# A two-block transformer layer on one core: the second block in three groups of tiles instead of two, its weights read three times

## The chip, the cores and the metric

The kernel runs on one core of a Trainium2 chip. The metric is the device time of one execution in microseconds; the median of three runs before the change is 2220.45 us. Five engines work side by side: TensorE (PE, matrix products; its weight loads are listed as PEld), VectorE (DVE), ScalarE (ACT), GpSimd (POOL, which here issues the gathers) and SyncE (SP, which issues the other transfers).

## The reference, cut to what matters

The input is 512 tokens of width 1024, float32. The first block ends in a layer that looks up experts; the second block is a projection, two mixers and an output product:

```python
# first block, last layer: for each token 8 heads x 16 experts = 128 rows of u and of v
uc = u[ic]
act = jnp.einsum("cd,ced->ce", xc, uc)
hid = gelu(act) * gc
return jnp.einsum("ce,ced->cd", hid, v[ic])
...
# second block
proj = rmsnorm_2(x, norm_pre) @ w_in                      # 1024 x 6416
xbc, dt_raw, z_ssd, sc_h, sc_b, sc_c, z_sc = split(proj)
xbc = silu(causal_dwconv(xbc, ssd_conv_w, ssd_conv_b))    # 4 taps along the tokens
y_ssd = rmsnorm_2(ssd_chunked(xbc, softplus(dt_raw + dt_bias), ...) * silu(z_ssd), ssd_norm)
y_sc = sc_b * causal_dwconv(sc_c * sc_h, sc_conv_w) * silu(z_sc)
x = x + rmsnorm_2(concatenate([y_ssd, y_sc]) @ w_out, norm_post)
return x + sigmoid(x @ w_ple_gate) * (p_i @ w_ple_proj)
```

The scan `ssd_chunked` runs over chunks of 128 tokens and carries a state from one chunk to the next, and both convolutions carry a few last columns, so the second block takes the token tiles in order.

## The kernel before, in words

The 512 tokens are four tiles of 128. Attention and the first block's products come first; the second block's own begin at 1185.6 us, when the gathers of tiles 0 and 1 are through. The expert rows are fetched by 512 gathers (line 269), one per tile and expert slot: each brings 128 rows of 2048 numbers, 1.049 MB, into one of six buffers `g`. VectorE multiplies the u half with the tokens and sums (line 271), ScalarE takes the gelu (276), VectorE builds two small diagonals `dg` (280), and TensorE adds the v half into `acc` (285). When a tile's 128 gathers are through, `folded` adds the sums to `xres` and sets `pre[t]`, which the second block needs to begin that tile.

The gathers are a generator, `peers`. The class `Paced` counts the columns that the other products stream, and each time `every` columns have been emitted it steps the generator once, which emits two gathers with their work; `steps_now` steps it without other work, and `drain` runs it out. Every engine works in the order of the program that a scheduler made of this, so the place of a gather's products among TensorE's other products is fixed.

The second block is `block_c(tiles)`, called for tiles 0 and 1 and, after the drain, for tiles 2 and 3. Its parts, by the names that the profile shows: `xbc` (10 blocks of 128 columns of the projection, each followed by a convolution on VectorE), `z` (8 blocks), the scan (`dt`, `acs`, `xsT`, `bm`, `cb`, `al`, `ys`, `st`, `sn`), `sc` (32 blocks in fours), `mix` (the output product, 16 blocks) and `pg` with `pp` (8 and 2 blocks). A block of weights is 512 KB, loaded by `wtile` (line 206) into one of four buffers. Except in `mix` of tiles 0 and 1 and in `pp`, `halves` splits it into two parts of a shorter format, the high part by a cast on ScalarE (353) and the low part by a subtraction on VectorE (354), and each product is three products of parts. `rows` keeps 128 x 128 of the weights stationary and streams the tokens of the group; `cols` keeps 128 tokens stationary and streams 512 columns of weights. In the second call a pool `px` adds a third buffer for the split weights and a split copy `yc` of the mixers' output.

```python
NG = 256
PACE_B, PACE_Q, PACE_C = 13600, 10500, 4600
...
block_c([0, 1])
T.drain()
gathering.close()
with pool("px") as px:
    block_c([2, 3], px)
```

Of the kernel before, what the change touches and what calls it, by code (L numbers as in the profile page):

```python
# [8 lines left out]
F32 = mybir.dt.float32  # L9
# [4 lines left out]
AF = mybir.ActivationFunctionType  # L14
# [3 lines left out]
P = 128  # L18
# [9 lines left out]
def _blocks(w, nb):  # L28
    return np.ascontiguousarray(w.reshape(8, P, nb, P).transpose(2, 1, 0, 3))


def _moving(w, n):
    k, c = w.shape
    kk = 1024 // n
    w = w.reshape(k // (kk * P), kk, P, c // n, n).transpose(3, 0, 2, 1, 4)
    return np.ascontiguousarray(w)
# [47 lines left out]
def layout(inp):  # L84
    f = {k: np.asarray(v) for k, v in inp.items()}
    g = lambda n: f[n][0]
    x = f["x"][0]
    w = g("w_in")
    w2 = g("w_in_2")
    a = {}  # L90
    a["x"] = np.ascontiguousarray(x)
    a["xT"] = np.ascontiguousarray(x.T.reshape(8, P, S).transpose(1, 0, 2))
    a["wqa"] = _blocks(w[:, 0:512], 4)
    a["wka"] = _blocks(w[:, 512:1024], 4)
    a["wva"] = _moving(w[:, 1024:1536], 512)
    a["wqb"] = _blocks(w[:, 1536:2048], 4)
    kb = w[:, 2048:2176].reshape(1024, 2, 1, 64)
    a["wkb"] = _blocks(np.broadcast_to(kb, (1024, 2, 2, 64)).reshape(1024, 256), 2)
    a["wvb"] = _blocks(w[:, 2176:2304], 1)
    a["wga"] = _blocks(w[:, 2304:3328], 8)  # L100
    a["wgb"] = _blocks(w[:, 3328:4352], 8)
    pj = np.stack([g("w_proj_a"), g("w_proj_b")])
    a["wgm"] = np.stack([_moving(w[:, 2304 + 1024 * i:3328 + 1024 * i], 512) for i in range(2)])
    a["wpm"] = np.stack([_moving(m, 512) for m in pj])
    a["wproj"] = np.ascontiguousarray(pj.reshape(2, 4, P, 8, P).transpose(3, 2, 0, 1, 4).reshape(8, P, 8, P))
    a["wout"] = _moving(g("w_out"), 512)
    a["wq"] = _blocks(g("peer_w_q"), 16)
    a["subk"] = np.ascontiguousarray(g("peer_sub_keys").reshape(16, P, P).transpose(2, 0, 1))
    a["uv"] = np.ascontiguousarray(np.concatenate([g("peer_u"), g("peer_v")], 1))
    a["nab"] = _na_bias(g("na_rpb"))  # L110
    sw = _swap()
    gq, gk = g("gqa_q_norm_g"), g("gqa_k_norm_g")
    a["gqk"] = np.ascontiguousarray(np.tile(np.stack([gq, gq[sw], gk, gk[sw]], 1), (2, 1)))
    a["n1"] = _col(g("norm1_g"))
    a["rows"] = np.ascontiguousarray(np.stack([g("norm2_g"), f["norm_f_g"], g("norm_pre_2"), g("norm_post_2")]))
    a["w2"] = _blocks(np.concatenate([w2[:, 0:1280], w2[:, 1296:]], 1), 50)
    a["wdt"] = np.ascontiguousarray(w2[:, 1280:1296].reshape(8, P, 16).transpose(1, 0, 2))
    a["cw"] = np.ascontiguousarray(g("ssd_conv_w_2").reshape(4, 10, P).transpose(2, 1, 0))
    a["cb"] = _col(g("ssd_conv_b_2"))
    a["scw"] = np.ascontiguousarray(g("sc_conv_w_2").reshape(3, 8, P).transpose(2, 1, 0))  # L120
    a["heads"] = np.ascontiguousarray(np.stack([g("dt_bias_2"), g("a_log_2")]))
    a["dsk"] = _col(np.repeat(g("d_skip_2"), 64))
    a["ssn"] = _col(g("ssd_norm_2"))
    a["wo2"] = _moving(g("w_out_2"), 512)
    a["wpg"] = _moving(g("w_ple_gate_2"), 512)
    a["wpp"] = _moving(g("w_ple_proj_2"), 512)
    p = g("p_2")[0]
    a["pT"] = np.ascontiguousarray(p.T.reshape(2, P, S).transpose(1, 0, 2))
    a.update(_tables())
    return a  # L130
# [43 lines left out]
def program(tc, a, out):  # L174
# [1 line left out]
    V, A, G, SP = nc.vector, nc.scalar, nc.gpsimd, nc.sync  # L176
    T = Paced(nc.tensor)
    first, rest = [0], [1, 2, 3]
    NG = 256
    PACE_B, PACE_Q, PACE_C = 13600, 10500, 4600  # L180

    with ExitStack() as ctx:
        cst = ctx.enter_context(tc.tile_pool(name="cst", bufs=1))
# [14 lines left out]
        def bank(name, tag="mm"):  # L198
            if tag in turns:
                turn[tag] = turn.get(tag, -1) + 1  # L200
                tag = turns[tag][turn[tag] % len(turns[tag])]
            return ps.tile([P, 512], F32, tag=tag, name=name, bufs=2 if tag in ("mm", "sb") else 1)
# [34 lines left out]
        def transpose4(dst, src):  # L237
            b = bank("tr")
            for i in range(4):
                T.transpose(b[:, i * P:(i + 1) * P], src[:, i * P:(i + 1) * P], idn)  # L240
            A.copy(dst, b.rearrange("p (a t) -> p a t", a=4))
# [606 lines left out]
        with tc.tile_pool(name="pc", bufs=1) as pc, tc.tile_pool(name="pd", bufs=2) as pd:  # L848
# [34 lines left out]
                    V.tensor_tensor(lo, b3, hi, op=OP.subtract)  # L883

            def block_c(tiles, px=None):
                n = len(tiles) * P
                last = tiles[-1] == NT - 1
                tags = ["p1", "a0", "a1"] if last else ["sb", "p1"]
                turns["mm"] = ["mm", "mm", "p0"]
# [46 lines left out]
                bT, cT = xsT[:, 8, :], xsT[:, 9, :]  # L936
                ycat = pc.tile([P, 16, NG], F32, tag="ycat", name="ycat")

                for c in range(8):
                    b = bank("z")  # L940
                    rows(a["w2"][10 + c], hT2, b, n, wws)
                    A.activation(ycat[:, c, :n], b[:, :n], AF.Tanh, scale=0.5)
                    V.scalar_tensor_tensor(ycat[:, c, :n], ycat[:, c, :n], 1.0, b[:, :n], op0=OP.add, op1=OP.mult)
# [118 lines left out]
                        A.copy(yc[:, 0, 0:8, tk], ycat[:, 0:8, tk])  # L1062
                        V.tensor_tensor(yc[:, 1, 0:8, tk], ycat[:, 0:8, tk], yc[:, 0, 0:8, tk], op=OP.subtract)

                for c in range(8):
                    bb = {}
                    for j in (0, 2, 3, 1):
                        bb[j] = bank("sc4", "mm" if j in (0, 3) else "sb")
                        rows(a["w2"][18 + 8 * j + c], hT2, bb[j], n, wws)
                    bh, bbm, bcm, bz = (bb[j] for j in range(4))  # L1070
                    hs = pd.tile([P, NG], F32, tag="hs", name="hs")
                    A.copy(hs[:, :n], bh[:, :n])
                    v = pd.tile([P, 2 + NG], F32, tag="raw", name="v")
                    V.tensor_copy(v[:, 0:2], halo2[:, c, :])
                    V.tensor_tensor(v[:, 2:2 + n], hs[:, :n], bcm[:, :n], op=OP.mult)
                    V.tensor_copy(halo2[:, c, :], v[:, n:n + 2])
                    o = ycat[:, 8 + c, :n]
                    V.tensor_scalar(o, v[:, 0:n], scw[:, c, 0:1], None, op0=OP.mult)
                    for j in range(1, 3):
                        V.scalar_tensor_tensor(o, v[:, j:j + n], scw[:, c, j:j + 1], o, op0=OP.mult, op1=OP.add)  # L1080
                    A.activation(hs[:, :n], bz[:, :n], AF.Tanh, scale=0.5)
                    V.tensor_tensor(o, o, bbm[:, :n], op=OP.mult)
                    V.scalar_tensor_tensor(hs[:, :n], hs[:, :n], 1.0, bz[:, :n], op0=OP.add, op1=OP.mult)
                    V.scalar_tensor_tensor(o, o, 0.5, hs[:, :n], op0=OP.mult, op1=OP.mult)
                    if px:
                        A.copy(yc[:, 0, 8 + c, :n], o)
                        V.tensor_tensor(yc[:, 1, 8 + c, :n], o, yc[:, 0, 8 + c, :n], op=OP.subtract)
# [31 lines left out]
                        SP.dma_start(out[t * P:(t + 1) * P, hsl], gt)  # L1119

            block_c([0, 1])
            T.drain()
            gathering.close()
            with pool("px") as px:
                block_c([2, 3], px)

# [15 lines left out]
```

## Time and profile before

| | |
|---|---|
| median of 3 runs | 2220.45 us (2219.86 to 2221.79) |
| profiled execution | 2217.67 us, of which the span is 2215.8 us |
| busy in the span | PE 1851.5 us (84%), DVE 1628.1 (73%), ACT 735.1 (33%), POOL 598.8 (27%) |
| transfers | 711.71 MB, mean 321 GB/s; the gathers' queue 536.90 MB |
| chain that ended last | PE 36%, DMA 25%, DVE 24%; largest line: the gathers' landing, 23% |

A busy share is an average over stages that have different limits, so the table does not say what a change in one stage is worth. For that the span is cut at the places where TensorE goes from one part of the second block to the next, and each stretch is read by itself: which engine or whether the transfers are full there.

### The profile page before, as it was taken

The numbers are of one execution on the slowest core, as the hardware profiler recorded it, in microseconds if no ns is written. First come the engines' busy times: TensorE is split into PE (matmuls) and PEld (weight loads), VectorE is DVE, ScalarE is ACT, GpSimd is POOL, SyncE is SP. The second block draws the span as 40 slices with busy tenths as digits, with TensorE's granted clock in tenths as the row PEclk, the third lists the DMA queues.
The fourth block names the chain that finished last, engine by engine and source line by source line (L and its number), as shares of the span: only waits on it lengthen the run. The fifth ranks groups of instructions, "written<-read, shape, count | busy, mean of one in ns | idle before, by whom it ended". The sixth has DMA issues, their size and how long they took to land.

```text
span 2215.8 us, 29509 instructions
## 1 busy us (share of the span) xinstructions
PE 1851.5 (84%) x10292; PEld 1032.5 (47%) x10292; DVE 1628.1 (73%) x4007; ACT 735.1 (33%) x1471; POOL 598.8 (27%) x520
## 2 busy tenths in 40 slices
PE   7998699899999898656648886896899866799998
PEld 5767445444444654001104552462453421298896
DVE  5376986788885966888868887886775766687865
ACT  4374265566501421111123342321220310154443
POOL 0000223333331233444433334433423333200000
PEclk9999789999999998656758997998999976699999
DMA  5366979889997899999989989899999999653363
GB/s 211 127 228 216 363 288 344 335 325 350 346 381 273 316 378 394 380 380 397 362 306 346 418 365 396 335 418 420 406 415 416 402 416 421 276 170 97 119 189 121
DMA packets 127316, 711.71 MB, mean 321 GB/s; under 512 B 15168, under 2 KB 18752, under 8 KB 61248
## 3 DMA queue, kind: packets, MB, share of 16 engines
q0 software_dynamic: 73728, 536.90, 60.6%
q1 hardware_dynamic: 53440, 172.92, 22.1%
q8 instruction: 83, 1.36, 0.2%
q14 instruction: 65, 0.53, 0.1%
HBM read 707.67 MB, written 2.10 MB: 320 GB/s over the span
## 4 chain that ended last, share of the span: by engine, by line
PE 36%; DMA 25%; DVE 24%; issue 7%; ACT 6%; POOL 1%; another core or an unknown queue 0%; DVEq 0%; POOLq 0%; ACTq 0%; SPq 0%
DMA g<-in_uv,idx 23%; DVE g L271 9%; PE sc L168 5%; PE acc L285 4%; PE mix L168 3%; PE pq L168 2%; PE ga L168 2%; PE z L168 2%; DVE dg L280 2%; PE pg L168 2%; PE ys L168 2%; DVE ww L354 2%; POOL g L269 1%; DVE own L295 1%; PE xbc L168 1%
## 5 line engine op out<-in xcount | busy, mean ns | idle before, releaser
L269 POOL DMA_INDIRECT g<-in_uv,idx x512 | 595.0, 1162 | 1297.7 <-PE acc L285 610.2
L285 PE MATMUL acc<-g,dg 64*64 64x512 f32 x3584 | 626.5, 755 | 249.9 <-DVE dg L280 229.8
L271 DVE SCALAR_TENSOR_TENSOR g<-g,xnp 128x1024 f32<-128x1024 f32 x512 | 624.7, 1221 | 188.2 <-DMA g<-in_uv,idx 181.9
L285 PEld LDWEIGHTS acc<-g,dg 64*64 64x64 f32 x3584 | 122.9, 154 | 621.0 <-DVE dg L280 492.8
L276 ACT ACTIVATE act<-act 128x1 f32<-128x1 f32 (+1 forms) x448 | 90.8, 203 | 945.7 <-DVE g L271 912.2
L354 DVE TENSOR_TENSOR ww<-w,ww 128x1024 fp32r<-128x1024 f32 x175 | 213.4, 1222 | 76.4 <-ACT ww L353 74.5
L280 DVE TENSOR_SCALAR dg<-two,act,gate 128x64 f32<-128x64 f32 x512 | 172.1, 351 | 132.6 <-ACT act L276 129.9
L353 ACT CAST ww<-w 128x1024 fp32r<-128x1024 f32 x175 | 182.2, 1044 | 172.8 <-PE sc L168 63.6
L168 PEld LDWEIGHTS sc<-hT,ww 128*128 128x128 f32 x1536 | 190.0, 193 | 54.0 <-issue 44.5
L168 PE MATMUL sc<-hT,ww 128*128 128x256 f32 x1536 | 206.1, 289 | 6.0 <-ACT fold L333 3.2
L168 PE MATMUL pq<-xT,w 128*128 128x128 f32 (+1 forms) x768 | 127.8, 323 | 0.6 <-DMA w<-in_wq 0.6
L168 PEld LDWEIGHTS pq<-xT,w 128*128 128x128 f32 x768 | 112.0, 200 | 19.8 <-issue 12.2
L295 DVE SCALAR_TENSOR_TENSOR own<-g,hid,own 128x512 f32<-128x512 f32 x127 | 95.1, 749 | 2.3
L168 PE MATMUL ga<-h,w 128*128 128x384 f32 x256 | 93.1, 513 | 2.8 <-DVE rot L411 2.8
L276 ACT ACT_TABLE_LOAD x61 | 78.3, 1283 | 18.1 <-DVE g L271 16.3
L168 PE MATMUL xbc<-hT,ww 128*128 128x256 f32 x480 | 64.2, 290 | 6.2 <-DVE ww L354 3.3
L168 PEld LDWEIGHTS xbc<-hT,ww 128*128 128x128 f32 x480 | 59.3, 192 | 20.4 <-issue 9.5
L168 PEld LDWEIGHTS ga<-h,w 128*128 128x128 f32 x256 | 48.7, 198 | 37.6 <-issue 8.3
L168 PE MATMUL q<-h,w 128*128 128x128 f32 (+1 forms) x256 | 61.1, 394 | 3.4 <-ACT rsq L407 3.4
L168 PE MATMUL mix<-w,ycat 128*128 128x512 f32 x128 | 61.5, 612 | 0.0
L168 PEld LDWEIGHTS z<-hT,ww 128*128 128x128 f32 x384 | 46.9, 190 | 12.3 <-issue 10.5
L168 PE MATMUL z<-hT,ww 128*128 128x256 f32 x384 | 50.5, 287 | 1.5 <-ACT raw L928 1.3
(338 smaller groups left out, 2269.8 us busy)
## 6 DMA issues: line engine op xcount, KB each, us to landing
w<-in_w SPq DMA_DIRECT2D x100, 512.0 KB
w<-in_wq SPq DMA_DIRECT2D x48, 512.0 KB
w<-in_wo SPq DMA_DIRECT2D x32, 512.0 KB
w<-in_wgm SPq DMA_DIRECT2D x16, 512.0 KB
w<-in_wout SPq DMA_DIRECT2D x16, 512.0 KB
g<-in_uv,idx POOLq DMA_INDIRECT x512
w<-in_wpg SPq DMA_DIRECT2D x16, 512.0 KB
w<-in_wqa SPq DMA_DIRECT2D x8, 512.0 KB
```

The source lines that it names most:

```text
L168: return self.count(max(n, 128) * (4 if rhs.dtype == F32 else 1), self.tensor.matmul(out, lhsT, rhs, **kw))
L269: G.indirect_dma_start(out=g.rearrange("p a d -> p (a d)"), out_offset=None, in_=a["uv"], in_offset=bass.IndirectOffsetOnAxis(ap=hk_idx[t] ...
L271: V.scalar_tensor_tensor(g[:, 0, :], g[:, 0, :], 1.0, xnp, op0=OP.mult, op1=OP.mult, accum_out=act[:, j % grp:j % grp + 1])
L276: A.activation(act[:, :grp], act[:, :grp], AF.Gelu)
L280: V.tensor_scalar(dg[:, m, :], two[:, 1, :], act[:, m:m + 1], gate[:, m:m + 1], op0=OP.mult, op1=OP.mult)
L285: T.tensor.matmul(acc[i][o, :], w, v, start=(e0 + j + 1 == grp), stop=(e0 + j + grp >= P), tile_position=(64 * i, 64 * m), skip_group_chec ...
L295: V.scalar_tensor_tensor(own, g[:, 1, HALVES[1]], hid[:, j:j + 1], own, op0=OP.mult, op1=OP.add)
L353: A.copy(ww[:, 0], w)
L354: V.tensor_tensor(ww[:, 1], w, ww[:, 0], op=OP.subtract)
```

## The change

`block_c` is called three times: for tiles 0 and 1, for tile 2, and for tile 3. The gathers of tile 2 are stepped at one step per 7960 columns (before: 4600) beside tiles 0 and 1 and then run until tile 2 is ready; the gathers of tile 3 are stepped at 5800 beside tile 2; what is left is drained, and tile 3 runs last, with `px`. Each call reads all of the block's weights (50 + 16 + 8 + 2 blocks of 512 KB).

In a call with one tile, `z` and `sc` go through `cols`, from a second layout of the same weights, `w2m`: 128 tokens are stationary and 512 columns of weights move. The results then have tokens on the partitions and are turned by TensorE (`transpose4`, and two transposes `vT` per `sc` step). `xbc` stays in `rows`, now with 128 columns of tokens moving in place of 256. `mix` of tile 2 is in full float32, as that of tiles 0 and 1.

```diff
+    sc = w2[:, 2320:].reshape(1024, 4, 8, P)[:, (0, 2, 3, 1)].transpose(0, 2, 1, 3).reshape(1024, 4096)
+    a["w2m"] = _moving(np.concatenate([w2[:, 1296:2320], sc], 1), 512)
...
-    NG = 256
-    PACE_B, PACE_Q, PACE_C = 13600, 10500, 4600
+    PACE_B, PACE_Q, PACE_C, PACE_D = 13600, 10500, 7960, 5800
...
-                n = len(tiles) * P
+                n = NG = len(tiles) * P
...
-                for c in range(8):
+                for half in range(2 if len(tiles) == 1 else 0):
+                    b = bank("z")
+                    cols([b], hT2, [(i, a["w2m"][half, i]) for i in range(4)], wws)
+                    zt = pd.tile([P, 512], F32, tag="m", name="zt")
+                    A.activation(zt, b, AF.Tanh, scale=0.5)
+                    V.scalar_tensor_tensor(zt, zt, 1.0, b, op0=OP.add, op1=OP.mult)
+                    transpose4(ycat[:, 4 * half:4 * half + 4, :], zt)
+                for c in range(8 if len(tiles) > 1 else 0):
                     b = bank("z")
                     rows(a["w2"][10 + c], hT2, b, n, wws)
...
-                for c in range(8):
+                for c in range(8 if len(tiles) == 1 else 0):
+
+                    b = bank("sc4")
+                    cols([b], hT2, [(i, a["w2m"][2 + c, i]) for i in range(4)], wws)
+                    bh, bcm, bz, bbm = (b[:, j * P:(j + 1) * P] for j in range(4))
+                    vo = pd.tile([P, 2, P], F32, tag="hs", name="vo")
+                    gt = pd.tile([P, P], F32, tag="gt", name="gt", bufs=1)
+                    A.copy(vo[:, 0, :], bh)
+                    V.tensor_tensor(vo[:, 0, :], vo[:, 0, :], bcm, op=OP.mult)
+                    A.activation(gt, bz, AF.Tanh, scale=0.5)
+                    V.scalar_tensor_tensor(gt, gt, 1.0, bz, op0=OP.add, op1=OP.mult)
+                    V.scalar_tensor_tensor(vo[:, 1, :], gt, 0.5, bbm, op0=OP.mult, op1=OP.mult)
+                    tb = sbank("vT")
+                    for j in range(2):
+                        T.transpose(tb[:, j * P:(j + 1) * P], vo[:, j, :], idn)
+                    v = pd.tile([P, 2 + NG], F32, tag="raw", name="v")
+                    V.tensor_copy(v[:, 0:2], halo2[:, c, :])
+                    A.copy(v[:, 2:2 + n], tb[:, 0:P])
+                    V.tensor_copy(halo2[:, c, :], v[:, n:n + 2])
+                    o = ycat[:, 8 + c, :]
+                    V.tensor_scalar(o, v[:, 0:n], scw[:, c, 0:1], None, op0=OP.mult)
+                    for j in range(1, 3):
+                        V.scalar_tensor_tensor(o, v[:, j:j + n], scw[:, c, j:j + 1], o, op0=OP.mult, op1=OP.add)
+                    V.tensor_tensor(o, o, tb[:, P:2 * P], op=OP.mult)
+                    if px:
+                        A.copy(yc[:, 0, 8 + c, :], o)
+                        V.tensor_tensor(yc[:, 1, 8 + c, :], o, yc[:, 0, 8 + c, :], op=OP.subtract)
+                for c in range(8 if len(tiles) > 1 else 0):
...
             block_c([0, 1])
+            while 2 not in pre:
+                T.steps_now(1)
+            T.every = PACE_D
+            block_c([2])
             T.drain()
             gathering.close()
             with pool("px") as px:
-                block_c([2, 3], px)
+                block_c([3], px)
```

What the pace does on TensorE, in the `sc` part of tiles 0 and 1. Four products `acc` are one gather; `sc_` with a number is one bank of an `sc` step. Before:

```order
L168 MATMUL sc_11418<-hT_7735,ww 128x256 x10
L285 MATMUL acc<-g,dg 64x512 x4
L168 MATMUL sc_11418<-hT_7735,ww 128x256 x11
L168 MATMUL sc_11470<-hT_7735,ww 128x256 x6
L285 MATMUL acc<-g,dg 64x512 x4
L168 MATMUL sc_11470<-hT_7735,ww 128x256 x11
L285 MATMUL acc<-g,dg 64x512 x4
```

and with the change:

```order
L170 MATMUL sc_10754<-hT_7735,ww 128x256 x2
L286 MATMUL acc<-g,dg 64x512 x3
L170 MATMUL sc_10754<-hT_7735,ww 128x256 x22
L170 MATMUL sc_10806<-hT_7735,ww 128x256 x24
L286 MATMUL acc<-g,dg 64x512 x4
L170 MATMUL sc_10858<-hT_7735,ww 128x256 x2
L286 MATMUL acc<-g,dg 64x512 x4
```

Fewer gathers stand between the same `sc` products: some 1.2 per block of weights in place of some 1.9.

The second place is TensorE where the gathers end and the last group begins. Here `fold` is `folded` of tile 3 and `tr` turns the normed tokens `scr`. Before:

```order
L168 MATMUL pg<-ww,x4T 128x512 x16
L285 MATMUL acc<-g,dg 64x512 x4
L168 MATMUL pg<-ww,x4T 128x512 x12
L285 MATMUL acc<-g,dg 64x512 x224
L321 MATMUL fold<-parts,two 64x512 x4
L171 MATMUL tr<-idn,scr 128x128 x8
```

and with the change (`pg` is now tile 2's):

```order
L286 MATMUL acc<-g,dg 64x512 x8
L170 MATMUL pg<-ww,x4T 128x512 x6
L286 MATMUL acc<-g,dg 64x512 x44
L322 MATMUL fold<-parts,two 64x512 x4
L170 MATMUL pp<-w,pT 128x512 x4
L173 MATMUL tr<-idn,scr 128x128 x8
L170 MATMUL pp<-w,pT 128x512 x2
L170 MATMUL xbc<-hT_14540,ww 128x128
```

Before, 56 gathers (224 products) come with nothing between them; now 11 do, and the products of tile 2 stand among the others.

The third place is VectorE in the scan of tile 2, which had no gathers beside it before:

```order
L355 TENSOR_TENSOR ww<-w,ww 128x1024
L281 TENSOR_SCALAR dg<-two,act,gate 128x64
L272 SCALAR_TENSOR_TENSOR g,act<-g,xnp 128x1024
L355 TENSOR_TENSOR ww<-w,ww 128x1024
L1037 SCALAR_TENSOR_TENSOR yz<-xsT,dsk,ys 128x128 x4
L1053 TENSOR_TENSOR st<-st,etot 64x512
L281 TENSOR_SCALAR dg<-two,act,gate 128x64
L272 SCALAR_TENSOR_TENSOR g,act<-g,xnp 128x1024
```

The subtraction of the split weights (355), the two gather steps (272, 281) and the scan's own steps now stand in one row on VectorE.

## Rows read from the trace of the kernel before

**Rows 1.** The page, part 2: 40 equal slices of the span (55.4 us each).

```profile
PE   7998699899999898656648886896899866799998
PEclk9999789999999998656758997998999976699999
DMA  5366979889997899999989989899999999653363
```

**Rows 2.** Windows: stretch (us), busy us and count of PE, PEld, DVE, ACT, POOL; PEclk, DMA share, GB/s.

```profile
1185.60:1246.80 61.20, 52.91 (x385) 35.29 (x385) 53.55 (x119) 18.28 (x45) 20.24 (x18) 0.97 0.94 377
1246.80:1290.50 43.70, 42.18 (x326) 28.97 (x325) 37.62 (x81) 15.95 (x34) 17.30 (x14) 1.00 1.02 418
1290.50:1426.60 136.10, 103.66 (x651) 47.79 (x651) 106.25 (x241) 50.22 (x90) 51.48 (x44) 0.85 0.91 361
1426.60:1515.00 88.40, 81.81 (x619) 53.89 (x617) 71.50 (x143) 24.47 (x53) 35.90 (x29) 1.00 1.00 407
1515.00:1563.00 48.00, 30.76 (x152) 6.82 (x152) 33.83 (x62) 6.67 (x26) 19.04 (x19) 0.72 1.01 415
1563.00:1645.20 82.20, 74.91 (x552) 48.97 (x553) 65.81 (x133) 23.25 (x54) 30.04 (x27) 0.98 1.01 412
1645.20:1733.00 87.80, 87.04 (x346) 27.95 (x344) 45.30 (x84) 7.36 (x31) 29.57 (x28) 1.00 1.01 416
1733.00:1792.00 59.00, 51.03 (x257) 26.26 (x256) 41.64 (x76) 21.23 (x42) 19.53 (x17) 0.91 1.01 404
1792.00:1919.20 127.20, 82.00 (x401) 13.71 (x400) 81.47 (x152) 12.11 (x52) 47.70 (x47) 0.70 1.00 413
1919.20:1949.00 29.80, 25.98 (x119) 14.60 (x112) 19.70 (x50) 13.06 (x26) 0.00 (x0) 0.79 0.27 89
1949.00:2001.00 52.00, 50.70 (x427) 49.99 (x425) 44.70 (x98) 26.80 (x47) 0.00 (x0) 1.00 0.55 174
2001.00:2136.50 135.50, 135.50 (x1038) 121.60 (x1037) 103.58 (x213) 58.84 (x84) 0.00 (x0) 0.97 0.39 125
2136.50:2180.60 44.10, 44.10 (x194) 35.86 (x192) 22.34 (x22) 20.43 (x25) 0.00 (x0) 1.00 0.60 190
2180.60:2215.80 35.20, 25.89 (x113) 21.06 (x112) 19.40 (x28) 13.16 (x19) 0.00 (x0) 0.94 0.24 77
```

**Rows 3.** Groups by line and shape, VectorE, 1185 to 1800 us.

```profile
L271 DVE SCALAR_TENSOR_TENSOR g<-g,xnp 128x1024 f32<-128x1024 f32 x194 | 236.7, 1221 | 68.0 <-DMA g<-in_uv,idx 63.9 <-PE acc L285 3.4
L354 DVE TENSOR_TENSOR ww<-w,ww 128x1024 fp32r<-128x1024 f32 x57 | 69.7, 1223 | 18.8 <-ACT ww L353 17.7 <-issue 0.8
L280 DVE TENSOR_SCALAR dg<-two,act,gate 128x64 f32<-128x64 f32 x194 | 68.2, 352 | 48.2 <-ACT act L276 47.2 <-issue 0.7
L271 DVE DVE_READ_ACCUMULATOR g<-g,xnp 128x1 f32 x193 | 15.9, 82 | 0.0
```

**Rows 4.** The same view, VectorE, 1921 to 2216 us.

```profile
L933 DVE SCALAR_TENSOR_TENSOR xsT<-raw,cw,xsT 128x256 f32<-128x256 f32 x30 | 14.1, 481 | 0.1
L1029 DVE SCALAR_TENSOR_TENSOR yz<-xsT,dsk,ys 128x128 f32<-128x128 f32 x16 | 4.5, 342 | 8.4 <-PE ys L168 8.4
```

**Rows 5.** The chain that ended last: start, us, engine, name, line, instructions.

```profile
719.62 3.57 PE pq L168 x32
...
1678.27 1.88 PE acc L285 x16
...
2032.45 3.05 PE dt L168 x24
...
2093.42 43.24 PE sc L168 x367
2136.65 44.18 PE mix L168 x192
```

**Rows 6.** Timeline: start, us, engine, line, operation; an early product, and the last gather's.

```profile
190.25 8.25 PE L168 MATMUL mf<-ww,mT 128*128 128x512 f32 x33
...
1919.24 1.23 DVE L271 SCALAR_TENSOR_TENSOR g<-g,xnp 128x1024 f32<-128x1024 f32 x1 [0.57 <-DMA g<-in_uv,idx]
```

## The prediction

> **What bounds the kernel now.** First the 40 slices [rows 1]: from the fifth to the thirty-fourth the transfers stand at 7 to 9 tenths or more, then they fall to 3 to 6 while TensorE goes to 7 to 9. So two limits stand one after the other: the gathers until about 1920 us, then a tail. Second the stretches of the second block [rows 2]. In the tail, 1919.2 to 2215.8 us (296.6 us, tiles 2 and 3), TensorE is busy nearly throughout and the transfers have a share of 0.24 to 0.60. In the nine stretches before (1185.6 to 1919.2, 733.6 us, 243 gathers by POOL's counts) the share is 1.00 to 1.02 in seven; it is 0.94 in the first (`xbc`), where VectorE has 53.55 of 61.2 us, and 0.91 in the third (the scan), where VectorE has 106.25 of 136.1. The ninth, 127.2 us with 47 gathers, is the drain. So the end is when the last gather lands (its work starts at 1919.24 [rows 6]) plus the tail after it. The change moves tile 2 out of the tail, and pays by a third reading of the weights among the gathers.
>
> **Part 1: the third reading.** 76 blocks of 512 KB are 39.8 MB. Full transfers moved 404 to 418 GB/s [rows 2]; I take 415, so the reading costs 96 us where transfers are full. The gathers are 1.049 MB each, 2.53 us. In the tail before, its own blocks came at a share of 0.6 at most, so that a reading there cost nothing; now one of the three is taken from the gathers.
>
> The Trainium skill, "DMA: Bandwidth & Descriptors", section "Where 436 GB/s comes from", says that between HBM and SBUF the HBM side binds, at about 358 GB/s per core. By it the third reading would be 111 us, 15 more than by the rows. The trace does not agree: 413 GB/s over the 127 us of the drain [rows 2], so the measurement decides.
>
> **Part 2: tiles 0 and 1, paced at 7960.** Only the number of gathers in each part changes, counted in the new order: 13, 7, 32, 35, 28 and 21 beside `xbc`, `z`, scan, `sc`, `mix` and the rest up to tile 2's first product. A gather costs VectorE 1.22 + 0.35 + 0.08 = 1.65 us [rows 3] and TensorE 0.94 us (16 records, two gathers, in 1.88 us [rows 5]). Stage by stage:
> - `xbc`: VectorE was the limit; 5 gathers less take 8 us from 53.55, and at the same 87% busy that is 53 us (before 61.2).
> - `z`: the transfers need 28 us now; 192 products at 118 ns (367 in 43.24 us [rows 5]) are 23 us, seven gathers 7, the `dt` products 3: 36 us with small waits (43.7).
> - scan: 12 gathers less at 2.5 us: 106 us (136.1). Transfers need some 83.
> - `sc`, 30 blocks: before, three stretches with 75 gathers took 218.6 us. With 35: transfers 126 us, TensorE 85 + 33 = 118, VectorE (171 in the three stretches, less 40 gathers of 1.65) 105. Two near the limit: 130 us.
> - `mix`: 28 gathers as before, 88 us. The rest, 21 gathers and 10 blocks, transfers full: 66 us.
>
> Sum 479 us: tile 2's first product at 1664.6 us.
>
> **Part 3: tile 2 beside the gathers of tile 3.** 107 gathers remain: 15, 12, 39, 18, 12 and 11.
> - `xbc`: a VectorE step on 128 columns runs each 0.28 us (16 in 4.5 us of busy time, against 30 in 14.1 on 256 [rows 4]). A block is one subtraction of 1.22 us and a convolution of some 1.7: ten are 29 us, 15 gathers 25. 54 on VectorE, 51 on the transfers: 57 us. TensorE's 128-column price stands in no row of this format. Below: 127 ns, the `dt` products with 16 columns (24 in 3.05 us [rows 5]), or 118 for 256. Above: 223 ns, full float32 at 128 columns (32 records, 16 products, in 3.57 us [rows 5]). I take 120, nearest to the format's own rows: 240 products are 29 us and the stage stays VectorE's; at 223 they are 54 and with 14 for the gathers 68 us.
> - `z`: 12 gathers and 8 blocks, transfers 40 us.
> - scan and `sc`: VectorE has 32 subtractions (39 us), eight `sc` steps of some 2.1 (17), one tile's scan (25, some 60 steps of 128 columns to 1024) and 39 gathers (64): 145 us. Transfers need 139. TensorE, with 192 products at 230 ns (192 in 44.18 us [rows 5]), is well below. Between 145 (no gaps) and 167 (87% busy, as in the first stretch of rows 2) I take 157.
> - `mix` 66, `pg` and `pp` 43, the last 11 gathers 28: all by the transfers. `mix` in float32, the transposes, the casts on ScalarE and the outputs on SP's queue lie beside them.
>
> Sum 391 us: the last gather's work at 2055.6 instead of 1919.2, **136.4 us later**. SP's queue gets no new wait ahead of weights that the tail needs: four buffers are filled while the last 11 gathers land.
>
> **Part 4: the tail with one tile.** Start: 29.8 us before, of which some 7 were the second tile's `pp` and `dt`: 23. `xbc` and `z`: VectorE 29 + 10 + 1 + 4 (the `dt` steps) = 44, TensorE 29 + 11: 48 us. Scan and `sc`: VectorE 39 + 19 + 25 = 83, TensorE 44 + 25 + 4: 89 us. `mix`: 16 blocks at 1.5 us, from the one stretch where single blocks of this form ran one after the other (33 products in 8.25 us [rows 6], six to a block): 24. End: 35.2 less half of `pg`: 25. Together **209 us**, 87.6 less than 296.6. VectorE, not TensorE, is the limit now: its 74 subtractions, 90 us, do not shrink with the tile. If VectorE were free, TensorE's sum of some 155 us would be next.
>
> **Sum.** +136.4 - 87.6 = +48.8 us. From the profiled execution's 2217.67 (span 2215.8 and 1.9 around it) that is 2266.5; the median of the runs lies 2.8 above it, so about 2269. I forecast 2268.
>
> **The rivals.**
> A. The transfers stay full through both groups. 243 gathers and some 153 blocks are 335 MB, 807 us at 415 GB/s, so the last gather's work starts at 1993 us, not 2056. With the tail of 209 the median is about 2206, and with a tail at VectorE's floor (170 us of work and 26 of waiting at its two ends, as in the first and last stretch of the tail [rows 2]) 2193. **This ends faster.** It decides where the time lost to unfull transfers in both groups stays below 14 us. For it: `sc` and `mix` run at 1.00 to 1.01 with VectorE 80% busy. Against: before, 733.6 us held 297 MB, 715 us at 415, so 19 us were lost already, and the change brings more VectorE work per transferred byte.
> B. The loss stays at those 19 us: +5 us, the median about 2225, at the edge of what can be told from no change; with a tail a few us shorter it is within 0.2%, which is about what a measurement of this kernel can tell from no change.
> C. The 128-column products cost 223 ns. Then `xbc` is TensorE's in both places: +11 us beside the gathers (68 against 57) and some +14 in the tail (54 + 11 against 48, less a few that VectorE makes up in `z`): the median about 2293. For it: the format's cost on few columns is shown nowhere; against it: 16 columns take 127 ns, not more than 256.
> D. The order does not do what the text says, so that gathers remain for the drain. The new order shows 11 in place of 56 there, so nothing is given to this.
>
> **How the numbers follow.** Forecast 0.54, C 0.22, A 0.16, B 0.08 (of which half within 0.2% and a fourth on either side). Faster: 0.16 + 0.02 = 0.18. Same: 0.04, and 0.01 from the forecast's edge: 0.05. Slower: 0.77. The range goes down to 2202, which cuts off most of A, and up to 2315: C's 2293 with 10 for the scan at 87% busy and some 13 for a tail with 85% busy VectorE. The slower cases alone have 2230 to 2315.
>
> **What would show it.** Right: the last gather's work at about 2055 us; a transfer share of 0.85 to 0.95 in `xbc` and in the scan with `sc` of both groups, with VectorE at 87% or more there; no stretch of 127 us with gathers alone, but one of about 28; a tail of about 209 us with VectorE above 80% and TensorE below. Step by step: tile 2's first product near 1665 us; `xbc` on 128 columns at 120 ns each. Wrong: a last gather before 2000 us (A), a tail under 190 us or over 230, `xbc` products at over 200 ns (C), or TensorE still without a gap in the tail.

## The result, and the profile after

The change makes the kernel slower: 2286.14 us, median of 4 runs (2279.24 to 2300.41), against 2220.15 for the kernel before in the same job; ratio 1.0307, 95% interval 1.0271 to 1.0343. The forecast was 2268 us. The profiled execution took 2279.24 us, its span 2277.5, 61.7 more than before; the sum of the prediction was 48.8.

Part 2 of the page, to hold against [rows 1]:

```profile
PE   7898699899999796555569989999899987877997
PEclk9999789999999997666679989999896999996898
DMA  5366979888996999999989978999996989996665
```

The transfers now fall after the thirty-sixth slice instead of the thirty-fourth, and the thirty-first slice (1708 to 1765 us) shows something that the prediction did not have: the clock at 6 while TensorE is at 9 or more. Cut at the same places as [rows 2]: first tiles 0 and 1 (`xbc`, `z`, scan, `sc`, `mix`, the rest), then tile 2 (`xbc`, `z`, scan and `sc`, `mix`, `pg`, drain), then the tail (start, `xbc` and `z`, scan and `sc`, `mix`, end). The last three rows are tiles 0 and 1, tile 2 and the tail, each as a whole. Columns: stretch in us, busy us and count of PE, PEld, DVE, ACT, POOL; PEclk, DMA share, GB/s.

```profile
1184.60:1238.80 54.20, 49.52 (x348) 34.11 (x348) 46.49 (x108) 16.86 (x39) 20.20 (x14) 0.97 0.89 348
1238.80:1275.20 36.40, 35.75 (x270) 28.23 (x271) 32.21 (x76) 15.55 (x31) 10.77 (x8) 1.00 0.95 375
1275.20:1379.10 103.90, 88.65 (x560) 43.57 (x558) 81.08 (x186) 38.01 (x67) 36.87 (x32) 0.93 0.82 312
1379.10:1517.70 138.60, 135.92 (x1003) 98.81 (x1002) 112.00 (x218) 42.17 (x84) 45.00 (x36) 1.00 0.98 389
1517.70:1609.00 91.30, 88.40 (x370) 29.72 (x372) 48.83 (x89) 7.11 (x32) 33.53 (x28) 1.00 1.00 407
1609.00:1675.80 66.80, 60.00 (x301) 29.05 (x293) 54.33 (x101) 31.22 (x60) 25.75 (x20) 0.90 0.96 388
1675.80:1755.40 79.60, 71.89 (x377) 46.87 (x373) 58.32 (x141) 17.59 (x50) 21.86 (x17) 0.68 0.82 326
1755.40:1794.50 39.10, 36.38 (x173) 15.72 (x172) 24.80 (x49) 14.04 (x24) 13.11 (x12) 0.91 0.89 351
1794.50:1934.10 139.60, 119.24 (x639) 57.89 (x636) 121.55 (x258) 60.51 (x111) 48.00 (x38) 0.99 0.97 390
1934.10:2000.00 65.90, 53.17 (x218) 15.50 (x218) 31.23 (x66) 5.82 (x26) 20.02 (x19) 0.95 1.02 416
2000.00:2044.50 44.50, 34.18 (x164) 14.62 (x156) 33.45 (x55) 14.68 (x27) 14.39 (x13) 0.88 1.02 417
2044.50:2074.70 30.20, 16.51 (x81) 2.84 (x80) 16.74 (x30) 4.29 (x12) 5.89 (x5) 0.63 0.90 373
2074.70:2093.60 18.90, 13.40 (x43) 5.15 (x40) 11.86 (x25) 8.06 (x19) 0.00 (x0) 0.59 0.35 110
2093.60:2142.30 48.70, 47.08 (x319) 44.52 (x319) 35.88 (x100) 23.82 (x41) 0.00 (x0) 0.86 0.54 171
2142.30:2217.80 75.50, 70.41 (x336) 51.50 (x334) 68.09 (x140) 48.41 (x73) 0.00 (x0) 0.95 0.66 216
2217.80:2251.80 34.00, 28.20 (x105) 19.21 (x103) 25.18 (x43) 20.44 (x29) 0.00 (x0) 0.95 0.76 261
2251.80:2277.50 25.70, 14.77 (x56) 11.05 (x56) 15.34 (x19) 11.48 (x15) 0.00 (x0) 0.81 0.36 125
1184.60:1675.80 491.20, 458.25 (x2840) 263.50 (x2840) 374.94 (x774) 150.92 (x313) 172.13 (x136) 0.97 0.94 370
1675.80:2074.70 398.90, 331.38 (x1637) 153.44 (x1633) 286.09 (x595) 116.92 (x248) 123.26 (x103) 0.87 0.94 380
2074.70:2277.50 202.80, 173.86 (x853) 131.43 (x849) 156.35 (x322) 112.20 (x175) 0.00 (x0) 0.88 0.58 191
```

The last gather's work, the counterpart of [rows 6], from the timeline of VectorE:

```profile
2074.72 1.22 DVE L272 SCALAR_TENSOR_TENSOR g<-g,xnp 128x1024 f32<-128x1024 f32 x1
```

It starts 155.5 us later than before (forecast 136.4), and the tail after it takes 202.8 us, 93.8 less (forecast 87.6). Before, the gathers' nine stretches lost 19 us to unfull transfers; now 890.1 us at 370 and 380 GB/s hold what at 415 would take some 803, so about 87 us are lost. In tiles 0 and 1 TensorE is the busiest engine (458 of 491 us) and is taken for the limit; no run relieved it there. In tile 2 no engine is full over the group, and one stretch stands out: `xbc`, 79.6 us where 57 were forecast, with TensorE busy 71.9 at a granted clock of 0.68. Its timeline shows when the clock fell (start, us, engine, line, operation; behind it the idle time before):

```profile
1689.28 1.78 PE L170 MATMUL xbc<-hT,ww 128*128 128x128 f32 x14
...
1693.62 1.09 PE L286 MATMUL acc<-g,dg 64*64 64x512 f32 x8 [0.83 <-DVE dg L281]
1694.64 0.77 PE L170 MATMUL xbc<-hT,ww 128*128 128x128 f32 x5
1697.57 1.99 PE L286 MATMUL acc<-g,dg 64*64 64x512 f32 x8 [2.15 <-DVE dg L281]
...
1721.48 0.69 PE L170 MATMUL xbc<-hT,ww 128*128 128x128 f32 x2 [2.97 <-ACT ww L354]
...
1730.41 6.66 PE L170 MATMUL xbc<-hT,ww 128*128 128x128 f32 x30
```

TensorE waits for `dg`, VectorE's last step for a gather, with the next `xbc` products behind the waiting `acc` in its queue; from 1697 on the same eight `acc` take 1.99 us instead of 1.09, and an `xbc` product 222 ns instead of 127 (6.66 / 30, 1.78 / 14). From 1713.8 the clock is back for a few microseconds (28 products in 3.71 us); then comes a wait of 2.97 us for the cast of a block of weights, and from 1722 to the end of the stretch the clock stays down, although TensorE is busy:

```profile
1722.10:1755.40 33.30, 32.49 (x127) 22.20 (x126) 23.05 (x60) 7.68 (x21) 5.11 (x4) 0.50 0.56 200
```

Until 1722 the transfers are full (415 GB/s or more), so it is this second fall that costs: at 1.2 GHz TensorE is what the stretch waits for, buffers come free late (of GpSimd's waits in these 33 us, 16.5 are put down to `acc` and 10.0 to VectorE), and the share over the whole stretch falls to 0.82. That the waits bring the clock down is read from the order in time, and from e5 and e12 below, where TensorE waits for nothing in this stretch and the clock stays at 1.00.

### The profile page after: what moved, and what is told of

It is laid out like the page before. It is cut to its first block, busy times and chain, and to the rows that moved or that the text cites. A ratio compares the mean times of both kernels' runs of the same rounds, so it can differ in the third digit from the quotient of the medians.

```text
span 2277.5 us, 29504 instructions
## 1 busy us (share of the span) xinstructions
PE 1915.4 (84%) x10068; PEld 1042.7 (46%) x10068; DVE 1700.6 (75%) x4202; ACT 803.8 (35%) x1584; POOL 621.6 (27%) x520
## 5 line engine op out<-in xcount | busy, mean ns | idle before, releaser
L270 POOL DMA_INDIRECT g<-in_uv,idx x512 | 617.8, 1207 | 1429.0 <-PE acc L286 745.0
L355 DVE TENSOR_TENSOR ww<-w,ww 128x1024 fp32r<-128x1024 f32 x233 | 283.4, 1221 | 69.1 <-ACT ww L354 66.4
L354 ACT CAST ww<-w 128x1024 fp32r<-128x1024 f32 x233 | 241.8, 1043 | 134.3 <-PE sc L170 27.2
L170 PE MATMUL sc<-ww,hT 128*128 128x512 f32 x384 | 110.1, 421 | 14.0 <-DVE ww L355 11.1
L170 PEld LDWEIGHTS xbc<-hT,ww 128*128 128x128 f32 x720 | 101.0, 222 | 39.0 <-issue 16.4
L170 PE MATMUL xbc<-hT,ww 128*128 128x128 f32 (+1 forms) x720 | 107.0, 312 | 9.1 <-ACT ww L354 7.0
L170 PEld LDWEIGHTS sc<-hT,ww 128*128 128x128 f32 x768 | 94.8, 192 | 34.4 <-issue 18.7
L170 PE MATMUL sc<-hT,ww 128*128 128x256 f32 x768 | 103.1, 289 | 3.1 <-ACT ww L354 3.0
L170 PE MATMUL mix<-w,ycat 128*128 128x512 f32 x192 | 94.1, 622 | 5.8 <-DMA w<-in_wo 5.8
L170 PEld LDWEIGHTS sc<-ww,hT 128*128 128x128 f32 x384 | 70.8, 194 | 56.4 <-DVE ww L355 20.3
```

The costliest lines, as they stand in the source:

```text
L170: return self.count(max(n, 128) * (4 if rhs.dtype == F32 else 1), self.tensor.matmul(out, lhsT, rhs, **kw))
L270: G.indirect_dma_start(out=g.rearrange("p a d -> p (a d)"), out_offset=None, in_=a["uv"], in_offset=bass.IndirectOffsetOnAxis(ap=hk_idx[t] ...
L354: A.copy(ww[:, 0], w)
L355: V.tensor_tensor(ww[:, 1], w, ww[:, 0], op=OP.subtract)
```

## The experiments

Ratios are to the kernel before, measured beside each. The theory at the outset: transfers are full, so the third reading costs its own 96 us, and unfull transfers the rest. Rival 1: the reading hides, and the loss alone is the cost. Rival 2: the pace is the cause.

**e1, the change without the third reading.** While tile 2 runs, `wtile` returns the first block of each shape.

```diff
+            if one[0] is not None and n in one[0]:
+                return one[0][n]
...
+            one[0] = {}
             block_c([2])
+            one[0] = None
```

> The three groups as in the change, but tile 2's group loads one block of weights of each shape and uses it 74 times: the third reading (39 MB) is left out, so tile 2's output is not the reference's; casts, subtractions and products stay. Theory (transfers are full, so the reading costs its own time): tile 2's group falls from 399 us to what VectorE and TensorE leave, about 60 (xbc) + 30 (z) + 130 (scan and sc) + 50 (mix) + 35 (pg) + 28 (drain) = 333 us, 66 less; the time about 2213 us, 0.997 of the kernel before. Rival 1 (the reading is hidden beside VectorE's work, and unfull transfers alone cost): no change against the three groups, 1.03. If all 96 us of the reading came back: 2183 us, 0.985.

Measured: 2271.25 us, 1.0217 (1.0200 to 1.0234). Both expectations miss. The group up to the last gather:

```profile
1677.40:2035.00 357.60, 331.62 (x1581) 153.18 (x1578) 272.66 (x583) 110.27 (x241) 120.02 (x102) 0.88 0.81 313
```

It falls by 41 us, not 66, with transfers at 0.81 and TensorE now busy 93%: the engines alone take nearly as long as the transfers. The half clock is part of that, for `xbc` is hardly shorter without the reading:

```profile
1677.40:1754.70 77.30, 71.22 (x377) 47.23 (x373) 58.59 (x142) 18.07 (x50) 20.13 (x16) 0.69 0.69 273
```

Of the 41, 30 us are given back behind the group: the tail takes 233.0 us in place of 202.8, its `xbc` 53 us at a clock of 0.51 (33 at 0.86 in the change).

**e2, the reading kept, the splitting away.** In tile 2's group the weights are not split, one product in place of three.

```diff
+            if not light[0]:
                 V.tensor_tensor(ww[:, 1], w, ww[:, 0], op=OP.subtract)
...
+                for x, y in PARTS[:1] if light[0] else PARTS:
```

> The three groups as in the change, with the third reading, but in tile 2's group the weights are not split: no subtraction on VectorE (58 of 1.22 us, 71 us) and one product of high parts in place of three. The low parts are left out, so tile 2 is less exact. Theory: 107 gathers and 76 blocks are 152 MB, 366 us at 415 GB/s, and now little else is in their way: tile 2's group about 375 us in place of 399, the transfers' share 0.97 or more in each of its stretches; the time about 2258 us, 1.017 of the kernel before. Rival 1 (the reading is hidden, VectorE's work sets the group): the group falls by most of VectorE's 71 us, to about 330, the time about 2210, 0.996.

Measured: 2264.54 us, 1.0191 (1.0151 to 1.0230), as the theory expected. The group is 374.7 us, at full transfers:

```profile
1680.40:2055.10 374.70, 264.11 (x1285) 92.80 (x1285) 225.09 (x537) 114.94 (x246) 113.42 (x103) 0.82 1.00 408
```

**e6, both edits together.**

```diff
+            one[0], light[0] = {}, True
             block_c([2])
+            one[0], light[0] = None, False
```

> The edits of e1 and e2 together: tile 2's group neither reads its weights nor splits them, one product in place of three (output not the reference's). Theory (two limits of about the same height, transfers at 366 us and the engines' work in order at about 360, so that taking one away brings little): with both away the group falls to its 107 gathers, 272 us and some 20 at its ends, 110 less than the 404 us in the change; the time about 2180 us, 0.98. Rival (something else sets the group, such as the six gather buffers): the group stays over 350 us, the time over 2235.

Measured: 2196.56 us, 0.9911 (0.9885 to 0.9937).

```profile
1677.50:1993.80 316.30, 269.89 (x1285) 100.19 (x1285) 222.33 (x537) 112.38 (x246) 107.71 (x103) 0.79 0.90 360
```

The group loses 82.6 us, more than the 41.3 and 24.2 of the single edits together. So two limits of nearly the same height stand over tile 2's group as it ran, some 366 us of transfers and 358 of engines in order with the half clock in them, and interleaved they give 399. The fall was expected as 110, so 27 us of it did not come; the transfers have a share of 0.90 there.

**e9, the reading by itself.** The kernel before, with 76 unused blocks loaded beside its last gathers.

```diff
             block_c([0, 1])
+            for i in range(76):
+                wtile(a["w2"][i % 50], P)
             T.drain()
```

> The kernel before with 76 more blocks of weights (39.8 MB) loaded and not used, between tiles 0 and 1 and the last group's own blocks, so that they come while the last gathers land and the engines are busy only 64% (VectorE and TensorE in that stretch). Theory (where nothing but the transfers limits, a reading costs its own time): the last gather 90 to 96 us later, 1.040 to 1.044 of the kernel before. Rival 1 (it goes beside the gathers for nothing): within 0.5%.

Measured: 2315.48 us, 1.0455 (1.0427 to 1.0484).

```profile
1792.00:1987.20 195.20, 101.71 (x424) 15.61 (x416) 87.45 (x157) 10.55 (x52) 68.23 (x50) 0.52 1.01 416
```

The last gather starts at 1987.2 us, 68 later and not the 90 to 96 expected, with the first 56 of the blocks (29.4 MB, 71 us at 415 GB/s) in the queue ahead of that; the other 20 came behind the gathers and held up the tail. Where only the transfers limit, the reading costs its own time: this term of the prediction stands.

**e4, the pace alone**, in the kernel before.

```diff
-    PACE_B, PACE_Q, PACE_C = 13600, 10500, 4600
+    PACE_B, PACE_Q, PACE_C = 13600, 10500, 7960
```

> The kernel before (two groups, weights read twice) with the one number of the pace beside tiles 0 and 1 changed from 4600 to 7960. Theory (at this pace TensorE, busy 458 of 491 us in the change, bounds tiles 0 and 1, and the transfers are not full there): tiles 0 and 1 take some 491 us as in the change, then 108 gathers of 2.54 us alone, 274 us: the last gather at about 1955 in place of 1919, the time about 2255 us, 1.016. Rival 2 (the transfers stay full at either pace, so what is not gathered beside is gathered in the drain): within 0.3% of the kernel before. Rival 1 has the same expectation as the theory.

Measured: 2237.00 us, 1.0066 (1.0045 to 1.0086): between the two.

```profile
1184.40:1669.00 484.60, 449.34 (x2817) 260.75 (x2818) 368.23 (x767) 148.02 (x310) 169.98 (x136) 0.98 0.94 373
1669.00:1943.40 274.40, 180.32 (x866) 29.93 (x868) 174.29 (x326) 24.20 (x110) 105.96 (x104) 0.70 1.00 415
```

The first row is the change's own tiles 0 and 1: TensorE busy 93%, transfers at 0.94. In the kernel before, the pace is worth 15 us, beside the 66 of the whole change, with the last gather 24 later.

**e7 and e8, more gathers ahead of tile 2**: the two paces are 6200 and 8500, then 5400 and 14000.

```diff
-    PACE_B, PACE_Q, PACE_C, PACE_D = 13600, 10500, 7960, 5800
+    PACE_B, PACE_Q, PACE_C, PACE_D = 13600, 10500, 6200, 8500
```

> The three groups as in the change, with the two paces 6200 and 8500 in place of 7960 and 5800: 8 more gathers ahead of tile 2's first product, 39 in its xbc in place of 15, and the last one before its mix. Theory (both groups have two limits near each other, so the order of gathers moves loss from one stretch to another): between 1.02 and 1.035 of the kernel before. Rival 2 (the pace is what costs): under 1.015.

> The same with 5400 and 14000: 45 more gathers ahead of tile 2's first product, the last one in the middle of its sc part. Theory: tiles 0 and 1 have full transfers again and take about 590 us, tile 2's group about 300; 1.02 to 1.035. Rival 2: under 1.015.

Measured: 2321.28 us, 1.0464 (1.0426 to 1.0503), and 2342.54 us, 1.0576 (1.0545 to 1.0607). Theory and rival both miss: it becomes slower. In e8 (`xbc` of tile 2, its scan and `sc`, its end, the tail's `xbc`, with the tail's start in the third):

```profile
1783.30:1920.30 137.00, 116.52 (x536) 62.15 (x533) 90.08 (x195) 21.20 (x67) 39.51 (x35) 0.62 0.83 330
1963.00:2057.90 94.90, 86.03 (x428) 47.67 (x426) 82.99 (x168) 57.62 (x85) 16.29 (x10) 1.00 0.80 296
2057.90:2130.50 72.60, 59.42 (x173) 30.58 (x173) 26.71 (x47) 22.35 (x38) 0.00 (x0) 0.93 0.70 226
2130.50:2186.00 55.50, 54.51 (x256) 54.42 (x257) 31.73 (x80) 16.46 (x31) 0.00 (x0) 0.51 0.39 123
```

The gathers that lag pile up in `xbc` (35 issued there in place of 17), where the clock is at 0.62; then none are left beside the rest of tile 2, and the transfers drop to 0.70 there. The tail's `xbc` runs at half clock too. In e7 the two are alike: `xbc` of tile 2 takes 164.5 us at 0.65 with 47 gathers issued in it, the tail's 55.3 us at 0.50. So neither run tells what the pace costs apart from the clock.

**e5, more products to keep the clock.** 12 overwritten products ahead of each `xbc` block of tile 2; the order of the gathers among the blocks stays.

```diff
+            for k in range(extra[0]):
+                for x, y in PARTS:
+                    T.tensor.matmul(b[:, :n], w[:, x, k, :], rhs[:, y, k, :n], start=True, stop=True)
```

> The three groups as in the change, with 12 more products of 128 columns ahead of each of the ten xbc blocks of tile 2, into the same bank and overwritten: 120 more, 13.6 us at 113 ns. In the change this stretch took 79.6 us with TensorE busy 71.9 at a granted clock of 0.68. Theory (TensorE waited for gathers, its clock fell to 1.2 GHz, and at 222 ns per product it became what the stretch waits for): more products fill the waits, the clock stays up, and the stretch takes 62 to 68 us, less than without them, with a granted clock over 0.9. Rival (TensorE has too much work there): TensorE's 72 us grow by 14 to 27, the stretch takes 93 to 106 us.

Measured: 2266.10 us, 1.0221 (1.0192 to 1.0250), faster than the change by doing more. Its `xbc` and `z` of tile 2, and one block:

```profile
1688.70:1747.20 58.50, 58.44 (x493) 45.47 (x489) 52.19 (x129) 16.70 (x45) 18.92 (x17) 1.00 1.02 418
1747.20:1778.90 31.70, 31.07 (x172) 15.37 (x171) 26.57 (x62) 14.46 (x26) 13.41 (x10) 1.00 1.01 411
```

```profile
1701.66 1.50 PE L371 MATMUL xbc<-hT,ww 128*128 128x128 f32 x12
1703.00 2.84 PE L170 MATMUL xbc<-hT,ww 128*128 128x128 f32 x24
```

58.5 us in place of 79.6 (expected 62 to 68) with 120 more products, clock 1.00 in place of 0.68, 118 ns a product, transfers full. The half clock was the stretch's limit. The whole group:

```profile
1688.70:2070.60 381.90, 317.50 (x1757) 153.82 (x1753) 286.22 (x595) 119.16 (x249) 118.57 (x103) 0.92 0.98 398
```

It is 17 us shorter than the change's. Of the 33 us by which that one lies above the transfers' 366, the half clock in `xbc` is thus about half. (In this profile tiles 0 and 1 took 13 us longer than in the change's.)

**e12, VectorE relieved in tile 2**: the subtractions left out, the three products kept; and **e11**, the same in the tail.

```diff
+            if lo[0]:
                 V.tensor_tensor(ww[:, 1], w, ww[:, 0], op=OP.subtract)
...
-                                T.matmul(b, lhs[:, x, k, tk], w[:, y, j, :], start=start and x + y == 0, stop=stop and x == 1)
+                                T.matmul(b, lhs[:, x, k, tk], w[:, y * lo[0], j, :], start=start and x + y == 0, stop=stop and x == 1)
```

> The same left out in tile 2's group in place of the last: 58 subtractions, 71 us of VectorE, with the third reading and TensorE's work as in the change. Theory (two limits: the transfers at 366 us, and TensorE's and VectorE's work in order with the gathers): the scan and sc, where the transfers have a share of 0.99, gain nothing; the group of 399 us loses at most 10; 1.026 to 1.031. Rival (VectorE sets the scan and sc, 121.6 of 139.6 us busy): the group loses 25 or more, 1.02 or less.

Measured: 2264.24 us (2254.06 to 2276.93, the profiled execution 2254.17), 1.0221 (1.0163 to 1.0279). Whole group, `xbc`, and scan with `sc`:

```profile
1675.70:2048.50 372.80, 297.85 (x1633) 138.75 (x1633) 226.44 (x536) 115.32 (x246) 116.25 (x103) 0.92 1.00 408
1675.70:1717.90 42.20, 42.20 (x353) 31.65 (x350) 32.95 (x100) 15.77 (x39) 13.58 (x14) 1.00 1.02 417
1750.00:1891.00 141.00, 116.17 (x607) 55.32 (x607) 88.47 (x212) 56.52 (x108) 43.22 (x38) 0.95 0.98 400
```

The scan and `sc` gain nothing with 33 us less on VectorE, as the theory has it; but the group gains 26 us, the rival's size, in a place that neither named: `xbc` takes 42.2 us at full clock, with 14 gathers issued in it in place of 17 and no wait of TensorE, and what stays is close to the transfers' time.

> The three groups as in the change, but in the last group the 74 subtractions of the split weights (90 us on VectorE) are left out and the products that used the low part of the weights use the high part again (so TensorE's work is the same; tile 3's output is not the reference's). Theory of the prediction (VectorE bounds the tail, TensorE's sum of some 155 us would be next; its busy time in the change's tail was 174 us): the tail falls from 203 us to 165 to 178; 1.013 to 1.020 of the kernel before. Rival (TensorE bounds it as much as VectorE): 190 us or more, 1.025 to 1.031.

Measured: 2263.86 us, 1.0202 (1.0170 to 1.0234).

```profile
2079.10:2260.90 181.80, 162.78 (x857) 124.38 (x849) 80.32 (x249) 111.11 (x175) 0.00 (x0) 0.93 0.64 212
```

Less than the theory wanted: the tail goes from 202.8 to 181.8 with TensorE busy 163. VectorE's subtractions hold the tail by 21 us, not by 25 to 38. Whether less work on TensorE alone would shorten it as well was not tried; in the change's tail TensorE is the busier of the two, 173.9 us to 156.4.

**e3, the form of `z` and `sc`**: the single tiles go through `rows`, 128 columns moving.

```diff
-                for half in range(2 if len(tiles) == 1 else 0):
+                for half in range(0):
...
-                for c in range(8 if len(tiles) > 1 else 0):
+                for c in range(8):
```

> The three groups as in the change, but z and sc of the single tiles go through the form of the large groups: weights stationary, 128 columns of tokens moving; no turning. Theory (at 113 ns for 128 columns and 230 for 512, this doubles TensorE's time for z and sc): the tail's scan and sc go from 87.5 to about 122 us and become TensorE's, z adds some 7; tile 2's scan and sc go from 140 to about 165, z by 8; together +75 us, 1.064 of the kernel before. Rival (VectorE sets both groups, so the moving form is worth nothing): 1.03, as with the change.

Measured: 2404.79 us, 1.0806 (1.0783 to 1.0829): the theory's sign, more than its size. The tail's `z`, and its scan and `sc`:

```profile
2188.00:2230.00 42.00, 42.00 (x198) 42.00 (x199) 15.06 (x32) 10.12 (x21) 0.00 (x0) 0.50 0.31 100
2230.00:2350.50 120.50, 120.50 (x902) 113.20 (x902) 79.43 (x172) 47.88 (x72) 0.00 (x0) 0.88 0.42 136
```

Scan and `sc` came to 120.5 us (expected 122); `z` took 42.0 against 17 in the change and some 25 expected, at half clock throughout. Tile 2's group lost more than estimated too: its last gather starts at 2128.5 us, 54 later than in the change (expected 33).

**e10, GpSimd takes every third subtraction of the tail.**

```diff
+                turned[0] += 1
+                e = G if turned[0] % 3 == 0 else V
+            e.tensor_tensor(ww[:, 1], w, ww[:, 0], op=OP.subtract)
```

> The three groups as in the change, but in the last group every third subtraction of the split weights (some 25 of 74, 1.22 us each on VectorE) is made by GpSimd, which has nothing to do there. Theory of the prediction (VectorE bounds the tail, 78.5 of 87.5 us busy in scan and sc): VectorE has 30 us less, the tail falls from 203 to 185 to 192 us; 1.022 to 1.026 of the kernel before. Rival (TensorE, 80.8 of 87.5 us there, bounds it as much): the tail stays within 5 us; 1.029 to 1.032. If GpSimd takes several times as long for one as VectorE, products wait for it and the tail is longer.

Measured: 2291.25 us, 1.0337 (1.0310 to 1.0364); no gain, so it says nothing on the tail's limit. VectorE lost its relief again: in the tail it is busy 159.9 us, 156.4 in the change, with 24 subtractions less. Its own steps became longer, as this group shows (from 2078 us; 344 ns each in the change):

```profile
L1100 DVE SCALAR_TENSOR_TENSOR ycat<-v,scw,ycat 128x128 f32<-128x128 f32 x16 | 11.7, 734 | 0.2
```

## Why the prediction was right, and where it was not

Sign and range held: 2286 is inside 2202 to 2315, and the case named likeliest (slower, since the third reading is taken from gathers at full transfers) is what happened. The nearness of the sum (61.7 us for 48.8) is in part luck: tiles 0 and 1 came 12 us longer, tile 2's group 8 longer and the tail 6 shorter, and inside the last two, misses of +22.6 and -17.4 (`xbc`, then scan and `sc`) and of -13.5 and +10.0 (the tail's scan and `sc`, then `mix`) cancel. By its steps:

- **Part 1, the reading at 96 us.** Right as a price where nothing else limits (e9: 68 us for 56 blocks). In tile 2's group it is a price in company: without it the group is only 41 us shorter, because the engines took 358 us anyhow. The sum of the prediction was saved by having taken the larger of the limits stage by stage; 96 as an addend would have been wrong.
- **Part 2, tiles 0 and 1 at 479 us.** 491.2. Five of six stretches are within 3.5 us; `sc` was mis-sized, 138.6 for 130, with TensorE busy 135.9 where 118 were counted: from the groups of that stretch, 720 products in 94.3 us are 131 ns each, not 118, and the `acc` of 35 gathers in 45.7 us are 1.31 us a gather, not 0.94 (280 records, 8 to a gather; the two groups overlap by some 5 us). e4 shows that this pace costs 15 us by itself in the kernel before.
- **Part 3, `xbc` of tile 2 at 57 us.** This is the step that failed: "I take 120 ... and the stage stays VectorE's". The products do run at 113 to 127 ns, but at 2.4 GHz alone. The prediction priced the form and not the clock, although [rows 2] show 0.70 to 0.85 in three stretches where TensorE was not busy throughout. Rival C had the size of the stage's product time (222 ns) for another reason. It cost 22.6 us, of which e5 gave back 21 in the stretch and 17 over the group.
- **Part 3, scan and `sc` at 157 us.** 139.6: VectorE's work was counted as 145 and was 121.6 busy, at the predicted 87%: added up by groups its instructions are 137 us, but their records overlap, which a sum of single durations leaves out. This hid most of the miss before it, by luck: the two errors cancel to 5 us. e12 shows that VectorE was not even the limit here, the transfers were (share 0.97).
- VectorE's durations from [rows 3] held (1.22, 0.35 and 1.22 us); a step on 128 columns took 0.34 to 0.35 us, not the 0.28 taken from [rows 4], where the row's own mean is 342 ns.
- The 243 gathers are not POOL's counts, which add up to 240 in [rows 2]; TensorE's records bear them out (1948 `acc` from 1185.6 to 1923 us, 8 to a gather), so the sums with 243 stand.
- `z`, `mix`, `pg` and the drain came to 39.1, 65.9, 44.5 and 30.2 for 40, 66, 43 and 28.
- **Part 4, the tail at 209 us.** 202.8. Scan and `sc` were 75.5 for 89, again VectorE's count (68 for 83), and `mix` 34.0 for 24, at a transfer rate of 261 GB/s: the sixteen blocks came at 2.1 us each, not 1.5. "VectorE, not TensorE, is the limit now" holds by 21 us as far as e11 shows it.
- **Rival A** fell by far: it needed under 14 us of lost transfer time, and some 87 were lost. Of these some 53 lie in tiles 0 and 1 at the new pace (491.2 us at 370 GB/s are 438 at 415) and some 34 in tile 2, of which e5 regained 17.
- **The signs.** The drain (30.2 us for 28), the tail's length and the transfer shares in `xbc` of tiles 0 and 1 came as named. VectorE at 87% or more with a share of 0.85 to 0.95 was seen nowhere: in tiles 0 and 1 it is busy 86% in `xbc` (share 0.89), 78% in the scan (0.82) and 81% in `sc` (0.98), in tile 2 73% in `xbc` (0.82) and 87% in the scan with `sc` (0.97). In the tail VectorE is at 77% and TensorE at 86%, where above and below 80% were named. And a sign of being wrong was there: `xbc` products of over 200 ns in the half-clock part of tile 2's `xbc` (222).

What stays open: the engines' 358 us in e1 contain the half clock in `xbc`; what the group would be without the reading and at full clock was not tried. With the reading and at full clock in `xbc` it took 381.9 us (e5). No version here beats the kernel before with the whole computation; e6 does, by leaving out what has to be computed.

## What to carry to other kernels

Before work is moved beside a transfer-bound phase, sum every engine's work in order there too: two limits of nearly the same height do not overlap for free, and here taking one away brought 41 or 24 us of the 83 that both brought. When a stretch shows a low granted clock and a busy TensorE, ask what it waited for before the clock fell; busy time at half clock is not a bound by work, and here adding products shortened the stretch by 21 us.

## What was not expected of the hardware

- **The clock without a wait.** In e3 the tail's `z` ran its 192 products of 128 columns in 41.20 us without a gap in the records, 215 ns each at a granted 0.50. In the change the tail's `xbc` ran at 1.00 from 2093.6 to 2115 us and at 0.58 in the next 15, busy throughout by the records. So a wait is not the only thing that goes before a fall; what else does is not shown, for e5 kept the clock with the same narrow products, there with a gather's `acc` of 512 columns between them. The Trainium skill, "TensorE: Matmul & The Clock Gate", section "HAM oscillation — how this bites in real kernels", lays a swinging clock to waits for data between short groups of products. Tile 2's `xbc` agrees in that waits stand ahead of both falls (0.83 and 2.15 us, then 2.97); e3's `z` does not show such waits.
- **VectorE and GpSimd stand in each other's way.** In e10 a step on 128 columns took 734 ns in place of 344 in the change's tail, and a subtraction that began while GpSimd was at its own 3.37 us in place of 1.22:

```profile
2165.45 2.87 POOL L359 TENSOR_TENSOR ww<-w,ww 128x1024 fp32r<-128x1024 f32 x1 [4.02 <-ACT ww L354]
2166.05 3.37 DVE L359 TENSOR_TENSOR ww<-w,ww 128x1024 fp32r<-128x1024 f32 x1
```

  The Trainium skill, "SBUF — State Buffer", section "Who interferes with whom", says that a VectorE instruction with two SBUF inputs contends with a GpSimd instruction that reads SBUF, over a pair of ports that is locked for one of them. This trace agrees: both instructions of the two rows above have two inputs in SBUF, and VectorE's ends 1.1 us after GpSimd's, about its own length. GpSimd took 2.46 us a subtraction (56.7 us for 23), twice VectorE's time.
- **The transfers.** One core moved 415 GB/s over 274 us of gathers (e4) and 416 over 195 us of gathers and weights (e9).
